# Forget gates of the second layer emitted beside band attention's third pair

## The chip, the cores and the metric

One core of a Trainium2 chip runs the whole program. Its engines work side by side, each through a queue of its own in fixed order: TensorE (PE) multiplies and transposes, VectorE (DVE), ScalarE (ACT) and GpSimd (POOL) do the elementwise work, and SyncE (SP) issues most of the DMA transfers. They wait for one another by semaphores. The metric is the device time of one execution in microseconds (us); lower is better.

## The reference

An encoder of two layers is run for 512 new frames of one stream (the prompt) and for the next 64 frames of another that has 1024 frames of history (the sample). The change lies in the second layer. Of its input projection the columns are cut into queries, keys, values and gates of two attentions of 8 heads each, "band" and "fox", and 8 columns for fox's forget values:

```python
q_c, k_c, v_c, g_c, q_d, k_d, v_d, f_d, g_d = split_cols(h @ w_in, ODD_SIZES)
log_f = jax.nn.log_sigmoid(f_d.astype(jnp.float32) + forget_bias.astype(jnp.float32))
...
cum = jnp.cumsum(log_f, axis=1)                                          # prompt
...
cum = jnp.cumsum(jnp.concatenate([p_lf.astype(jnp.float32), log_f], axis=1), axis=1)   # sample
...
s = s + (jnp.swapaxes(cum_q, 1, 2)[:, :, :, None] - jnp.swapaxes(cum_k, 1, 2)[:, :, None, :])
```

The running sums enter the scores of fox alone. `log_f` itself is an output.

## The kernel before

Every float32 product is made as three products of the operands' high and low parts, so a projection of one 128-wide tile is 48 matmuls: a bank of 256 frames (24 matmuls) and one of 320, the last 64 of them the sample's. Weights come by DMA into `wraw` (4 buffers); ACT makes the high part `whi` (L165) and POOL the low part `wlo` (L169), 5 buffers each.

The heads go by pairs, four for band and four for fox. For each pair there are projections (`band_qk` or `fox_qk`, matmuls at L252, evictions at L339 to L357), a gate tile (`gate_tile`, L252, evictions at L632 and L633), and the attention. The attention of a prompt pair (`head_out`) is a chain per 128 rows: scores (PE, L452, L453), bias and row minimum (DVE, L1227), exponential (ACT, L461), division (DVE, L463, L464), transposes (PE, L418), a split into two parts (ACT L421, DVE L422), then the product with the values (PE, L427). The sample's rows run beside it (L501 to L557). `v_chunk` projects two pairs' values, with matmuls at L262 (prompt) and L270 (sample).

What stands where is set twice. A scheduler orders each engine's queue by priority, and the attention of band and fox is emitted under a high one, so that projections emitted before or after it fill the places where the attention waits. Buffers of a ring, however, are handed out in the order in which the code asks for them. PSUM has two buffers each of `psA` (projections), `psS` (scores) and `psT` (transposes), one each of `psU` and `psX`. The ring "E" has five buffers of 2 KB rows, shared by `kf`, `kout`, `th`, `low`, `vf`, `cum` and `oT`.

The loop at L1278 runs over band's pairs p: `band_qk(p + 1)`, for p = 1 also the second value chunk, the gate tile, then the attention of pair p. Behind the loop stand fox's first value chunk (L1290) and the block that the change moves:

- the projection `w_vd1` of 264 columns: 256 values of fox and the 8 forget columns, four prompt tiles and the sample (96 and 16 matmuls), evicted at L1294, L1295, L282, L283, L1302, L1303;
- the logarithms (L1310 to L1319): ten small instructions on 128 x 40 numbers, turn by turn on ACT and DVE, with `Ln` at L1317, which needs a load of another ACT table, and two stores of the result (L1320, L1321);
- the running sums: PE transposes the log values into two `psT` banks (L1336, L1347), ACT copies them out (L1338, L1348), three loads bring the history's log values (`fox_lfT`, L1344), DVE makes one scan for the prompt and three chained ones for the sample (L1327), and each result is stored in DRAM (`cum_p`, `cum_s`, L1329).

Fox's attention reads them back as bias tiles `T` (`spread`, L1355). `fox_qk(0)` follows.

Of the kernel before, what the change touches and what calls it, by code (L numbers as in the profile page):

```python
# [10 lines left out]
F32 = mybir.dt.float32  # L11
F32R = mybir.dt.float32r
BF16 = mybir.dt.bfloat16
AF = mybir.ActivationFunctionType
ALU = mybir.AluOpType
AX = mybir.AxisListType

P = 128
D = 1024
KT = D // P  # L20
S = 512
NT = S // P
DS = 64
TT = S + DS
PAST = 1024
H = 8
# [33 lines left out]
def f32(ap):  # L60
    return ap.bitcast(F32)
# [3 lines left out]
def kernel(ctx: ExitStack, tc: tile.TileContext, a: dict, o: dict):  # L65
    nc = tc.nc
# [6 lines left out]
    dp = pool("dram", space=bass.MemoryType.DRAM)  # L73
# [3 lines left out]
    def nm(s):  # L77
        cnt[0] += 1
        return f"{s}_{cnt[0]}"
# [14 lines left out]
    def ring(shape, dt, tag, name=None):  # L94
        p, n = rings[tag]
        if isinstance(p, list):
            rings[tag][1] += 1
            return p[n % len(p)].tile(shape, dt, name=nm(name or tag), tag=tag, bufs=1)
        return p.tile(shape, dt, name=nm(name or tag), tag=tag, bufs=n)
# [4 lines left out]
    def Er(shape, name="e"):  # L104
        return ring(shape, F32, "E", name)
# [4 lines left out]
    def V2(shape, dt, name="v"):  # L110
        return ring(shape, dt, "V2", name)
# [4 lines left out]
    def bank(tag, bufs, n=512):  # L116
        return lambda: pp.tile([P, n], F32, name=nm("ps" + tag), tag=tag, bufs=bufs)

    psA, psS, psT, psU, psX = bank("A", 2), bank("S", 2), bank("T", 2), bank("U", 1), bank("X", 1)
# [5 lines left out]
    ident = cp.tile([P, P], F32, name="ident")  # L125
# [49 lines left out]
    def w_split(src, shape):  # L175
        return split(src, w_tile("wraw", shape, F32), w_tile("whi", shape, F32R), w_tile("wlo", shape, F32R))
# [45 lines left out]
    def bcast(src_row, n):  # L222
        return bass.AP(src_row.tensor, src_row.offset, [[0, P], [1, n]])
# [32 lines left out]
    def tm_prompt(ps, n, ws, h, ks, t):  # L256

        kp = KT // len(ws)
        for k in ks:
            hi, lo = ws[k // kp]  # L260
            for m, (x, w) in enumerate(((0, hi), (0, lo), (1, hi))):
                nc.tensor.matmul(ps[:, :n], h.m[k // 4][:, k % 4, x, t * P:(t + 1) * P], w[:, k % kp, :],  # L262
                                 start=(k == ks[0] and m == 0), stop=(k == ks[-1] and m == 2))

    def tm_sample(ps, n, ws, h, ks):

        kp = KT // len(ws)
        for k in ks:
            for m, w in enumerate(ws[k // kp]):
                nc.tensor.matmul(ps[:, :n], h.s[k // 4][:, k % 4, :], w[:, k % kp, :],  # L270
                                 start=(k == ks[0] and m == 0), stop=(k == ks[-1] and m == 1))

    def tm_chunk(ws, n, h, prompt_cb, sdst, ts=range(NT + 1)):

        for t in ts:
            ps = psA()
            if t < NT:
                tm_prompt(ps, n, ws, h, range(KT), t)
                prompt_cb(t, ps)
            else:  # L280
                tm_sample(ps, n, ws, h, range(KT))
                nc.scalar.copy(sdst, ps[DS:P, :n])  # L282
                nc.vector.tensor_add(sdst, ps[:DS, :n], sdst)  # L283

    def tm_weights(src):
        return [w_split(src[i], list(src[i].shape)) for i in range(4)]
# [99 lines left out]
    def put_v(dst, src):  # L386

        s4 = src.rearrange("p (a s d) -> p a s d", s=2, d=64)
        d4 = dst.rearrange("p a (s d) -> p a s d", s=4)[:, :, ::3, :]
        nc.vector.tensor_copy(out=d4, in_=s4)  # L390
        nc.vector.tensor_sub(dst[:, :, 64:192].rearrange("p a (s d) -> p a s d", s=2), s4, f32(d4))
# [226 lines left out]
    def gate_tile(src, h, ft, raw):  # L618
        g = bp.tile([P, TT], F32, name=nm("g"), tag=f"g{ft}", bufs=1)
        gates[ft] = g  # L620

        def cb(ps, c0, c1):
            n = c1 - c0
            gv = g[:, c0:c1]
            th = Er([P, 320], "th")
            tv = th[:, :n]
            if raw:
                nc.scalar.activation(tv, ps[:, :n], AF.Sigmoid)
                nc.vector.tensor_mul(gv, ps[:, :n], tv)
            else:  # L630

                nc.scalar.activation(tv, ps[:, :n], AF.Tanh, scale=0.5)  # L632
                nc.vector.scalar_tensor_tensor(out=gv, in0=tv, scalar=1.0, in1=ps[:, :n], op0=ALU.add, op1=ALU.mult)  # L633

        ws_tiles(h, ((src, cb, ()),))
# [134 lines left out]
    def load_x(t):  # L770
        rows = P if t < NT else DS
        x = [Rr([P, 512], "x") for _ in range(2)]
        for c in range(2):
            nc.sync.dma_start(f32(x[c][:rows]), xrow(t)[:, c * 512:(c + 1) * 512])
        return [f32(y) for y in x]
# [9 lines left out]
    x = load_x(0)  # L785
# [8 lines left out]
    for t in range(NT + 1):  # L794
# [7 lines left out]
        if t < NT:  # L802
            c0_weights(C0W[t])
            x = load_x(t + 1)
# [282 lines left out]
    t = psA()  # L1087
# [3 lines left out]
    for i in range(2):  # L1091
        raw = w_tile("wraw", [P, 512], F32)
        cs = slice(i * 512, (i + 1) * 512)
# [94 lines left out]
    h1 = new_h(big1)  # L1188
# [15 lines left out]
    l1 = new_pool(st_l1)  # L1204
    band, fox = new_mech(l1, "band"), new_mech(l1, "fox")
    fb = l1.tile([P, H], F32, name="fb")
    nc.scalar.dma_start(fb, bcast(a["d_forget_bias"], H))
    lf = l1.tile([P, NT + 1, H], F32, name="lf")
# [44 lines left out]
    def band_sample(p):  # L1253
# [10 lines left out]
                        lambda c: s_vals(a["band_v"][p], c, band.vn[:, p * P:(p + 1) * P]), s_new)  # L1264
        s_gate(s_fold(po, rs), gates[p])

    nc.sync.dma_start(npost, bcast(a["norm_post"][1:2, :], D))
    clear(band)
    clear_keys(band.kz)
# [8 lines left out]
    for p in range(NPAIR):  # L1278
        nxt = band_qk(p + 1) if p < 3 else None
        if p == 1:  # L1280
            v_chunk(band, 1, a["w_vc"][1], h1, o["p_bandv"])
        gate_tile(a["ws"][32 + p], h1, p, False)
        with tc.high_priority(PR_band):
            beside(band_sample(p), EV_band)
            band_pair(p, pr)
            drain()
        pr = nxt
    nc.sync.dma_start(o["s_bandv"][CL - DS:], band.vn)

    v_chunk(fox, 0, a["w_vd0"], h1, o["p_foxv"])  # L1290

    def vf_prompt(t, ps):
        vf = Er([P, 256], "vf")
        nc.scalar.copy(vf, ps[:, :256])  # L1294
        nc.vector.tensor_add(lf[:, t], ps[:, 256:264], fb)  # L1295
        nc.sync.dma_start(o["p_foxv"][t * P:(t + 1) * P, 256:], vf)
        fox.v[1, t] = V2([P, 2, 256], F32R)
        put_v(fox.v[1, t], vf)

    low = Er([P, 264], "low")  # L1300
    tm_chunk(tm_weights(a["w_vd1"]), 264, h1, vf_prompt, low[:DS])
    nc.vector.tensor_copy(out=fox.vn[:, 256:], in_=low[:DS, :256])  # L1302
    nc.vector.tensor_add(lf[:DS, NT], low[:DS, 256:264], fb[:DS])  # L1303
    nc.sync.dma_start(o["s_foxv"], fox.vn)


    lff = lf.rearrange("p t h -> p (t h)")
    NF = (NT + 1) * H
    e, u, w = (l1.tile([P, NF], F32, name=x) for x in ("lf_e", "lf_u", "lf_w"))
    nc.scalar.activation(e, lff, AF.Abs)  # L1310
    nc.scalar.activation(e, e, AF.Exp, scale=-1.0)
    nc.vector.tensor_scalar(out=u, in0=e, scalar1=1.0, scalar2=None, op0=ALU.add)
    nc.vector.tensor_scalar(out=w, in0=u, scalar1=-1.0, scalar2=None, op0=ALU.add)
    nc.vector.tensor_sub(e, e, w)
    nc.vector.reciprocal(w, u)
    nc.vector.tensor_mul(e, e, w)
    nc.scalar.activation(u, u, AF.Ln)  # L1317
    nc.vector.tensor_add(u, u, e)
    nc.vector.scalar_tensor_tensor(out=lff, in0=lff, scalar=0.0, in1=u, op0=ALU.min, op1=ALU.subtract)  # L1319
    nc.sync.dma_start(o["p_logf"].rearrange("(t p) h -> p t h", p=P), lf[:, :NT])  # L1320
    nc.sync.dma_start(o["s_logf"], lf[:DS, NT])  # L1321


    def running(parts, dst):
        carry, k = 0.0, 0
        for c, w in parts:
            nc.vector.tensor_tensor_scan(out=c[:H, :w], data0=c[:H, :w], data1=c[:H, :w], initial=carry,  # L1327
                                         op0=ALU.add, op1=ALU.bypass)
            nc.sync.dma_start(dst[:, k:k + w], c[:H, :w])  # L1329
            carry, k = c[:H, w - 1:w], k + w  # L1330

    cum_p = dp.tile([H, S], F32, name="cum_p")
    cum_s = dp.tile([H, PAST + DS], F32, name="cum_s")
    t = psT()
    for i in range(NT):
        nc.tensor.transpose(t[:H, i * P:(i + 1) * P], lf[:, i, :], ident)  # L1336
    c = Er([P, S], "cum")
    nc.scalar.copy(c[:H], t[:H])  # L1338
    running([(c, S)], cum_p)
    cs = []  # L1340
    for k in range(3):
        c = Er([P, 384], "cum")
        w = min(384, PAST - k * 384)
        nc.sync.dma_start(c[:H, :w], a["fox_lfT"][:, k * 384:k * 384 + w])  # L1344
        cs.append((c, w))
    t = psT()
    nc.tensor.transpose(t[:H, :DS], lf[:DS, NT, :], ident[:DS, :DS])  # L1347
    nc.scalar.copy(cs[2][0][:H, 256:256 + DS], t[:H, :DS])  # L1348
    cs[2] = (cs[2][0], 256 + DS)
    running(cs, cum_s)  # L1350

    def spread(dst, src, h, k0, n):

# [184 lines left out]
```

## Time and profile before

| | |
|---|---|
| runs | 835.79, 839.99, 846.00 us; median 839.99 |
| profiled execution | 844.3 us, of which the span of the trace is 842.5 |
| mean granted TensorE clock | 0.974 of full speed |
| PE busy | 776.0 us, 92% of the span |
| DVE busy | 506.7 us, 60% |
| ACT busy | 499.1 us, 59% |
| POOL busy | 380.1 us, 45% |

The engines overlap, so the busy times don't add up to the span. All times of single instructions below are from the profiled execution, counted from the start of its span; a matmul's own duration contains its way through the array, and consecutive ones overlap. Band's last pairs, the moved block and the start of fox lie between 540 and 670 us.

### The profile page before, as it was taken

What the parts mean: (1) busy time and instruction counts of PE and PEld (TensorE: products, weight loads), DVE (VectorE), ACT (ScalarE), POOL (GpSimd) and SP (SyncE); (2) the same over time, 40 slices, a digit from 0 to 9 for tenths busy, and PEclk for the clock granted to TensorE, in tenths of its full rate; (3) what the DMA queues carried; (4) which work ended last, traced back from release to release, by engine and by line L of the source; (5) the groups of instructions that cost most, each with busy time, mean ns of one, the idle gap of its engine ahead of it and who ended that gap; (6) DMA issues with size and microseconds to landing.
All of it is one profiled execution on the core that took longest, in us unless ns stands there. A gap on an engine that the chain in (4) does not pass through costs nothing. (4 is left out here: it accounts for less than half of the span.)

```text
span 842.5 us, 16286 instructions
## 1 busy us (share of the span) xinstructions
PE 776.0 (92%) x5581; PEld 720.4 (86%) x5581; DVE 506.7 (60%) x1318; ACT 499.1 (59%) x1342; POOL 380.1 (45%) x461
## 2 busy tenths in 40 slices
PE   7989999999998999889877999999997899999986
PEld 5879899999896888788876999999896799998986
DVE  4642755777855765837854555564754576658345
ACT  6643755677746675665543655575634767768521
POOL 6574533463417040154671545453245444546453
PEclk9989999999997999999998999999999999999999
DMA  8233423541123022246352544343233533551562
GB/s 244 76 112 96 141 68 107 182 124 55 43 78 100 23 52 78 60 122 213 113 160 69 154 106 116 110 133 88 70 95 102 180 123 110 159 140 56 164 213 100
DMA packets 69924, 95.52 MB, mean 113 GB/s; under 512 B 9529, under 2 KB 40489, under 8 KB 69810
## 3 DMA queue, kind: packets, MB, share of 16 engines
q1 hardware_dynamic: 69264, 94.12, 37.2%
q8 instruction: 44, 0.72, 0.3%
q10 hardware_dynamic: 578, 0.37, 0.1%
q14 instruction: 38, 0.31, 0.1%
HBM read 74.36 MB, written 18.79 MB: 111 GB/s over the span
## 5 line engine op out<-in xcount | busy, mean ns | idle before, releaser
L252 PE MATMUL psA<-hT,whi 128*128 128x320 f32 (+1 forms) x1216 | 259.1, 301 | 6.1 <-DVE r L340 2.2
L169 POOL TENSOR_TENSOR wlo<-wraw,whi 128x512 fp32r<-128x512 f32 (+2 forms) x130 | 167.6, 1299 | 196.6 <-ACT whi L165 155.0
L252 PEld LDWEIGHTS psA<-hT,whi 128*128 128x128 f32 x1216 | 198.6, 190 | 9.8 <-issue 4.1
L252 PE MATMUL psA<-hT,wlo 128*128 128x320 f32 (+1 forms) x608 | 183.3, 302 | 0.0
L262 PE MATMUL psA<-whi,hT 128*128 128x256 f32 (+2 forms) x812 | 163.8, 290 | 4.8 <-DVE m L737 2.2
L262 PEld LDWEIGHTS psA<-whi,hT 128*128 128x128 f32 x812 | 131.7, 191 | 7.2 <-DVE m L737 2.4
L262 PE MATMUL psA<-wlo,hT 128*128 128x256 f32 (+2 forms) x420 | 122.5, 292 | 0.0
L252 PEld LDWEIGHTS psA<-hT,wlo 128*128 128x128 f32 x608 | 115.6, 190 | 0.8
L165 ACT CAST whi<-wraw 128x512 fp32r<-128x512 f32 (+2 forms) x130 | 78.2, 615 | 42.1 <-PE psA L252 23.0
L262 PEld LDWEIGHTS psA<-wlo,hT 128*128 128x128 f32 x420 | 80.8, 192 | 0.8
L363 POOL TENSOR_TENSOR kz<-kf,r 64x256 fp32r<-64x256 f32 x48 | 36.6, 762 | 35.1 <-ACT kf L357 33.3
L422 DVE TENSOR_TENSOR pt1l<-psT,pt1h 128x384 fp32r<-128x384 f32 x64 | 39.7, 620 | 13.5 <-ACT pt1h L421 12.6
L1227 DVE CUSTOM_DVE_ANT_0 x<-psS,T 128x128 f32<-128x128 f32 (+1 forms) x64 | 31.0, 484 | 23.4 <-PE psT L418 8.5
L339 ACT ACTIVATE r<-psA 64x256 fp32r<-64x256 f32 x48 | 18.1, 378 | 41.1 <-PE psA L252 22.7
L533 POOL TENSOR_TENSOR sK<-kraw,sK 128x384 fp32r<-128x384 f32 (+2 forms) x32 | 30.1, 941 | 27.3 <-ACT sK L532 21.9
L461 ACT ACTIVATE psS<-x,st 128x128 f32<-128x128 f32 (+1 forms) x64 | 34.1, 532 | 13.7 <-DVE st L1227 13.3
L439 POOL TENSOR_TENSOR g<-g,oT 128x512 f32<-128x512 f32 x14 | 18.3, 1305 | 52.3 <-DVE oT L431 52.0
L421 ACT CAST pt1h<-psT 128x384 fp32r<-128x384 f32 x64 | 33.8, 530 | 13.3 <-PE psT L418 12.0
L520 PE MATMUL psX<-vs,sP 128*128 128x256 f32 (+1 forms) x184 | 38.6, 303 | 1.5 <-DVE sP L507 1.2
L431 DVE SCALAR_TENSOR_TENSOR oT<-psU,oT 64x256 f32<-64x256 f32 x64 | 26.8, 419 | 19.2 <-ACT oT L430 18.3
L452 PE MATMUL psS<-r,r 128*128 128x256 f32 (+1 forms) x96 | 35.1, 367 | 2.1 <-DVE st L1227 1.2
L430 ACT ACTIVATE oT<-psU 64x256 f32<-64x256 f32 x64 | 24.2, 378 | 21.7 <-PE psU L427 20.6
(390 smaller groups left out, 1915.6 us busy)
## 6 DMA issues: line engine op xcount, KB each, us to landing
wraw<-in_ws_dram SPq DMA_DIRECT2D x80, 256.0 KB
wraw<-in_w_out_dram SPq DMA_DIRECT2D x32, 256.0 KB
x<-in_x_prompt_dram SPq DMA_DIRECT2D x16, 256.0 KB
part<-part SPq DMA_DIRECT2D x32, 128.0 KB
m<-part SPq DMA_DIRECT2D x16, 256.0 KB
r<-r SPq DMA_DIRECT2D x48, 64.0 KB
out_dram<-kout SPq DMA_DIRECT2D x12, 256.0 KB
out_dram<-vf SPq DMA_DIRECT2D x24, 128.0 KB
```

Source lines behind the costliest of these rows:

```text
L165: nc.scalar.copy(hi, raw)
L169: eng.tensor_sub(lo, raw, f32(hi))
L252: nc.tensor.matmul(ps[:, :c1 - c0], w[:, k % 4, :], h.m[k // 4][:, k % 4, x, c0:c1], start=(k == 0 and n == 0), stop=(k == KT - 1 and n == 2))
L262: nc.tensor.matmul(ps[:, :n], h.m[k // 4][:, k % 4, x, t * P:(t + 1) * P], w[:, k % kp, :], start=(k == ks[0] and m == 0), stop=(k == ks[- ...
L363: nc.gpsimd.tensor_sub(pair.kl[s][me, cs], kf[me, cs], f32(k[me, cs]))
L421: nc.scalar.copy(ph[:, :i + 1, at], tv)
L422: nc.vector.tensor_sub(pl[:, :i + 1, at], tv, f32(ph[:, :i + 1, at]))
L452: nc.tensor.matmul(ps[:, :w], pair.qq[s][:, q], pair.kk[s][:, :w], start=True, stop=False)
L461: nc.scalar.activation(ps[:, :n], src, AF.Exp, bias=mn, scale=-1.0, accum_out=sm)
L520: nc.tensor.matmul(po[:, :256], l, r, start=(first and n == 0), stop=(last and n == len(ops) - 1))
L533: nc.gpsimd.tensor_sub(kl[:, :w], raw[:, :w], f32(kh[:, :w]))
L1227: nc.vector.tensor_tensor_reduce(out=x, in0=ps, in1=b, scale=1.0, scalar=3e38, op0=ALU.add, op1=ALU.min, accum_out=mn)
```

## The change

The block becomes a function `forget_gates()`, called in the loop over band's pairs at p = 2, behind that pair's gate tile and ahead of its attention. The two DRAM tiles and `vf_prompt` move up as they are. Inside, `running` now takes one chunk at a time: the load of `fox_lfT`, the scan and the store of a chunk are emitted in turn, and the carry is handed on. Fox's first value chunk now comes behind the second one, and so does the store `s_foxv` of the sample's values. The arithmetic is the same.

```diff
+    def forget_gates():
+        low = Er([P, 264], "low")
+        tm_chunk(tm_weights(a["w_vd1"]), 264, h1, vf_prompt, low[:DS])
...
+        nc.sync.dma_start(o["s_logf"], lf[:DS, NT])
+        def running(c, w, dst, k, carry):
+            nc.vector.tensor_tensor_scan(out=c[:H, :w], data0=c[:H, :w], data1=c[:H, :w], initial=carry,
+                                         op0=ALU.add, op1=ALU.bypass)
+            nc.sync.dma_start(dst[:, k:k + w], c[:H, :w])
+            return c[:H, w - 1:w]
+        t = psT()
+        for i in range(NT):
+            nc.tensor.transpose(t[:H, i * P:(i + 1) * P], lf[:, i, :], ident)
+        c = Er([P, S], "cum")
+        nc.scalar.copy(c[:H], t[:H])
+        running(c, S, cum_p, 0, 0.0)
+        carry = 0.0
+        for k in range(0, PAST, 384):
+            c = Er([P, 384], "cum")
+            w = min(384, PAST - k)
+            nc.sync.dma_start(c[:H, :w], a["fox_lfT"][:, k:k + w])
+            if k + w == PAST:
+                t = psT()
+                nc.tensor.transpose(t[:H, :DS], lf[:DS, NT, :], ident[:DS, :DS])
+                nc.scalar.copy(c[:H, w:w + DS], t[:H, :DS])
+                w += DS
+            carry = running(c, w, cum_s, k, carry)
...
         gate_tile(a["ws"][32 + p], h1, p, False)
+        if p == 2:
+            forget_gates()
         with tc.high_priority(PR_band):
...
     v_chunk(fox, 0, a["w_vd0"], h1, o["p_foxv"])
-    low = Er([P, 264], "low")
-    tm_chunk(tm_weights(a["w_vd1"]), 264, h1, vf_prompt, low[:DS])
...
-    running(cs, cum_s)
```

In the changed program the block's lines are L1275 for L1296, L1291 to L1300 for L1312 to L1321, L1304 for L1327, L1306 for L1329, L1311 and L1322 for L1336 and L1347, L1319 for L1344.

On PE, where the attention of band's third pair (p = 2) starts, its first transpose (the row L418) stood before among the projection of the fourth pair's queries:

```order
L427 MATMUL psU_7430<-pt0l,v_6136 128x256
L418 MATMUL psT_7773<-ident,x_7766 128x128
L252 MATMUL psA_7575<-hT_5393,whi_7564 128x256 x2
L452 MATMUL psS_7844<-r_6813,r_6810 128x384
L252 MATMUL psA_7575<-hT_5393,wlo_7565 128x256
L453 MATMUL psS_7844<-kz_5926,r_6810 128x384
```

Now four sets of scores of that pair stand ahead, then all of the block's 112 matmuls and the fourth pair's gate tile (the L252 rows) with nothing of the attention among them, and then this, with the first transpose behind those of the log values:

```order
L252 MATMUL psA_8247<-hT_5395,whi_8214 128x320 x2
L252 MATMUL psA_8247<-hT_5395,wlo_8215 128x320
L1311 MATMUL psT_7913<-ident,lf 8x128 x4
L1322 MATMUL psT_7932<-ident,lf 8x64
L418 MATMUL psT_7988<-ident,x_7981 128x128
L501 MATMUL psT_8001<-ident,sx_7940 128x128 x2
L520 MATMUL psX_7994<-vs_7998,sP_8004 128x256
L418 MATMUL psT_8023<-ident,x_8016 128x128 x2
```

The attention's transposes have changed places with the log values': they ask for `psT` banks behind them.

On DVE, the scans (printed as SCALAR_TENSOR_TENSOR) stood before among the evictions of fox's first queries:

```order
L1319 SCALAR_TENSOR_TENSOR lf<-lf,lf_u 128x40
L340 SCALAR_TENSOR_TENSOR r_8712<-psA_8758,r_8712 64x256
L345 SCALAR_TENSOR_TENSOR foxqbl<-psA_8758,foxqbh 64x64
L340 SCALAR_TENSOR_TENSOR r_8713<-psA_8758,r_8713 64x256
L1327 SCALAR_TENSOR_TENSOR cum_8690<-cum_8690 8x512
L345 SCALAR_TENSOR_TENSOR foxqbl<-psA_8758,foxqbh 64x64
L1327 SCALAR_TENSOR_TENSOR cum_8694<-cum_8694 8x384
L1327 SCALAR_TENSOR_TENSOR cum_8696<-cum_8696,cum_8694 8x384
```

Now they stand between rows of the third pair's softmax (the splits L422 and L507, the bias L1227):

```order
L1298 SCALAR_TENSOR_TENSOR lf<-lf,lf_u 128x40
L1304 SCALAR_TENSOR_TENSOR cum_7918<-cum_7918 8x512
L1227 ISA x_8092,st_8091<-psS_8088,T_7397 128x512
L1227 ISA st_8091 128x1
L422 TENSOR_TENSOR pt0l<-psT_7988,pt0h 128x128
L1304 SCALAR_TENSOR_TENSOR cum_7922<-cum_7922 8x384
L507 TENSOR_TENSOR sP_8005<-psT_8001,sP_8004 128x256
L1304 SCALAR_TENSOR_TENSOR cum_7926<-cum_7926,cum_7922 8x384
L463 RECIPROCAL st_8096<-st_8094 128x1
```

Each of the attention's rows there comes behind a scan.

On SP, the loads of the history's log values (L1319) stand behind the two stores of the new ones and a weight load for fox's first keys (`wraw_8797`):

```order
L160 DMA wraw_8791<-in_ws_dram 128x512
L1299 DMA out_dram<-lf 128x4x8
L1300 DMA out_dram<-lf 64x8
L160 DMA wraw_8797<-in_ws_dram 128x512
L1319 DMA cum_7922<-in_fox_lfT_dram 8x384
L1319 DMA cum_7926<-in_fox_lfT_dram 8x384
L1319 DMA cum_7930<-in_fox_lfT_dram 8x256
L1306 DMA cum_p<-cum_7918 8x512
L1217 DMA T_8288<-in_relb_dram 64x256 x2
```

Before, they stood behind the same stores and two later weight loads; behind them now wait bias rows of band's fourth pair (`T`, L1217).

## Rows read from the trace of the kernel before

**Rows 1.** Windows: stretch, its length, busy us (and instructions) by engine, PEclk, DMA.
```profile
592.39:598.07 5.68, 4.93 (x32) 3.76 (x31) 5.48 (x21) 4.62 (x15) 1.28 (x1) 1.00 0.04 10
598.07:625.67 27.60, 27.60 (x222) 26.79 (x221) 16.25 (x51) 13.57 (x36) 7.43 (x8) 1.00 0.30 90
625.67:649.19 23.52, 18.67 (x132) 16.66 (x131) 14.29 (x23) 11.51 (x28) 16.89 (x20) 1.00 0.30 88
649.19:662.00 12.81, 10.18 (x70) 9.35 (x71) 5.13 (x19) 7.13 (x18) 3.36 (x3) 1.00 0.68 203
```

**Rows 2.** Timeline of PE: start, duration, engine, line, operation, [idle before <-releaser].
```profile
625.54 0.29 PE L270 MATMUL psA<-wlo,hsT 128*128 128x264 f32 x1
625.67 0.40 PE L252 MATMUL psA<-hT,whi 128*128 128x256 f32 x2
628.50 0.45 PE L252 MATMUL psA<-hT,whi 128*128 128x320 f32 x2
631.86 0.31 PE L252 MATMUL psA<-hT,wlo 128*128 128x320 f32 x1
```

**Rows 3.** Groups of PE instructions by form, 625.67 to 662.
```profile
L252 PE MATMUL psA<-hT,whi 128*128 128x256 f32 x64 | 12.3, 288 | 2.3 <-DVE r L340 2.2
L252 PE MATMUL psA<-hT,whi 128*128 128x320 f32 x52 | 11.6, 311 | 2.0 <-DVE foxqbl L345 2.0
L252 PE MATMUL psA<-hT,wlo 128*128 128x256 f32 x32 | 9.2, 286 | 0.0
L252 PE MATMUL psA<-hT,wlo 128*128 128x320 f32 x25 | 7.7, 308 | 0.0
```

**Rows 4.** Waits of PE, 600 to 690: us in total, times, longest us.
```profile
PE psA L252 <- DVE r L340: 2.2, 2, 1.2
PE psA L252 <- DVE foxqbl L345: 2.0, 2, 1.3
PE psS L452 <- DVE st L1227: 1.2, 1, 1.2
PE psA L374 <- ACT kf L357: 1.1, 1, 1.1
```

**Rows 5.** Timeline of DVE, forget gates' chain and scans.
```profile
627.37 1.39 DVE L1302 COPY foxvn<-low 64x256 f32<-64x256 f32 x1
630.28 1.22 DVE L1313 TENSOR_SCALAR lf_w<-lf_u 128x40 f32<-128x40 f32 x1
631.52 0.42 DVE L340 SCALAR_TENSOR_TENSOR r<-psA,r 64x256 fp32r<-64x256 f32 x1
633.10 1.32 DVE L1316 TENSOR_TENSOR lf_e<-lf_e,lf_w 128x40 f32<-128x40 f32 x1
637.45 1.21 DVE L1327 TENSOR_TENSOR_SCAN cum<-cum 8x512 f32<-8x512 f32 x1 [0.17 <-ACT cum L1338]
639.80 0.95 DVE L1327 TENSOR_TENSOR_SCAN cum<-cum 8x384 f32<-8x384 f32 x1 [0.88 <-DMA cum<-in_fox_lfT_dram]
640.84 3.04 DVE L1327 TENSOR_TENSOR_SCAN cum<-cum,cum 8x384 f32<-8x384 f32 x2
```

**Rows 6.** Timeline of POOL in the same stretch.
```profile
628.90 2.55 POOL L169 TENSOR_TENSOR wlo<-wraw,whi 128x512 fp32r<-128x512 f32 x2
633.08 1.29 POOL L169 TENSOR_TENSOR wlo<-wraw,whi 128x512 fp32r<-128x512 f32 x1 [1.06 <-ACT whi L165]
```

**Rows 7.** Timeline of PE: transposes of the log values.
```profile
635.29 0.60 PE L1336 MATMUL psT<-ident,lf 128*8 128x128 f32 x4
```

**Rows 8.** Timeline of ACT: the copy out of PSUM.
```profile
636.84 0.57 ACT L1338 COPY cum<-psT 8x512 f32<-8x512 f32 x1
```

**Rows 9.** Windows of two us around a gap in layer 0, columns as in rows 1.
```profile
444.00:446.00 2.00, 0.61 (x6) 0.38 (x4) 1.93 (x5) 2.00 (x6) 0.00 (x0) 1.00 0.59 229
446.00:448.00 2.00, 0.00 (x0) 0.00 (x0) 1.30 (x3) 0.55 (x2) 0.86 (x2) 0.66 0.28 98
450.00:452.00 2.00, 2.00 (x9) 1.55 (x8) 1.38 (x2) 1.43 (x4) 0.18 (x1) 0.50 0.44 131
```

More of the change, by code (lines that the diff above doesn't have):

```diff
@@ L1265, in band_sample, with vf_prompt @@
         s_gate(s_fold(po, rs), gates[p])
+    cum_p = dp.tile([H, S], F32, name="cum_p")
+    cum_s = dp.tile([H, PAST + DS], F32, name="cum_s")
+    def vf_prompt(t, ps):
+        vf = Er([P, 256], "vf")
+        nc.scalar.copy(vf, ps[:, :256])
+        nc.vector.tensor_add(lf[:, t], ps[:, 256:264], fb)
+        nc.sync.dma_start(o["p_foxv"][t * P:(t + 1) * P, 256:], vf)
+        fox.v[1, t] = V2([P, 2, 256], F32R)
+        put_v(fox.v[1, t], vf)
+    def forget_gates():
+        low = Er([P, 264], "low")
+        tm_chunk(tm_weights(a["w_vd1"]), 264, h1, vf_prompt, low[:DS])
+        nc.vector.tensor_copy(out=fox.vn[:, 256:], in_=low[:DS, :256])
+        nc.vector.tensor_add(lf[:DS, NT], low[:DS, 256:264], fb[:DS])
+        lff = lf.rearrange("p t h -> p (t h)")
+        NF = (NT + 1) * H
+        e, u, w = (l1.tile([P, NF], F32, name=x) for x in ("lf_e", "lf_u", "lf_w"))
+        nc.scalar.activation(e, lff, AF.Abs)
+        nc.scalar.activation(e, e, AF.Exp, scale=-1.0)
+        nc.vector.tensor_scalar(out=u, in0=e, scalar1=1.0, scalar2=None, op0=ALU.add)
+        nc.vector.tensor_scalar(out=w, in0=u, scalar1=-1.0, scalar2=None, op0=ALU.add)
+        nc.vector.tensor_sub(e, e, w)
+        nc.vector.reciprocal(w, u)
+        nc.vector.tensor_mul(e, e, w)
+        nc.scalar.activation(u, u, AF.Ln)
+        nc.vector.tensor_add(u, u, e)
+        nc.vector.scalar_tensor_tensor(out=lff, in0=lff, scalar=0.0, in1=u, op0=ALU.min, op1=ALU.subtract)
+        nc.sync.dma_start(o["p_logf"].rearrange("(t p) h -> p t h", p=P), lf[:, :NT])
+        nc.sync.dma_start(o["s_logf"], lf[:DS, NT])
[21 more added lines that the diff above has]
+            carry = running(c, w, cum_s, k, carry)
@@ L1290 @@
     v_chunk(fox, 0, a["w_vd0"], h1, o["p_foxv"])
[L1292 to L1298, printed above, removed]
-    low = Er([P, 264], "low")
-    tm_chunk(tm_weights(a["w_vd1"]), 264, h1, vf_prompt, low[:DS])
-    nc.vector.tensor_copy(out=fox.vn[:, 256:], in_=low[:DS, :256])
@@ L1303 @@
-    nc.vector.tensor_add(lf[:DS, NT], low[:DS, 256:264], fb[:DS])
-    nc.sync.dma_start(o["s_foxv"], fox.vn)
[L1307 to L1349, printed above, removed]
-    running(cs, cum_s)
+    nc.sync.dma_start(o["s_foxv"], fox.vn)
     def spread(dst, src, h, k0, n):
```

## The prediction

> **What bounds the kernel now.** PE is busy nearly all the time, so I read the stretch around the moved block by PE alone: first the windows, which say how many matmuls each stretch gets through, then PE's timeline and waits, which say what stops it, then the queues of DVE, ACT and POOL behind the longest stop.
>
> The windows [rows 1] show three kinds of stretch. In 598.07 to 625.67, the projections of fox's values with band's last attention dissolved in them, PE has no gap: 222 matmuls in 27.60 us, 0.124 us each. In 592.39 to 598.07 attention stands bare, with no projection between its matmuls: 32 in 5.68 us, 0.178 each, while DVE is busy for 5.48 us of it with 21 instructions, 0.26 each. There DVE is the bound. And from 625.67 to 662.00, where the forget gates' logarithms and sums run beside fox's first projections, PE has gaps.
>
> How large these are: the projection's 256-column matmuls start 0.118 us apart (24 from 625.67 to 628.50) and the 320-column ones 0.146 apart (23 from 628.50 to 631.86) [rows 2]. In 625.67 to 662.00 there are 64 + 32 of the first and 52 + 25 of the second [rows 3], and 132 + 70 in all [rows 1], so 29 others. The work is 96 x 0.118 + 77 x 0.146 + 29 x 0.124 = 11.3 + 11.2 + 3.6 = 26.1 us of 36.33. So **10.2 us are idle**. What ends these waits is the eviction of fox's queries by DVE (2.2 and 2.0 us), a softmax row (1.2) and the eviction of keys by ACT (1.1) [rows 4]. The evictions are late because the forget chain stands ahead of them on the same engines: 1.39, 1.22 and 1.32 us for three DVE rows of the logarithms [rows 5], and 1.21 + 0.95 + 3.04 = 5.2 us of scans [rows 5]. In the bare stretch the same reckoning gives 5.68 - 32 x 0.124 = 1.7 us idle.
>
> **The change, part by part.** No arithmetic is added. The 112 matmuls, the logarithms, the four scans and the table load for the logarithm run once in either kernel. So the sum is over PE's idle time, from band's third pair to the start of fox.
>
> *Taken away.* The hole of 10.2 us loses the forget chain. What stays is what fox's start has for itself: the keys' eviction (1.1), the first softmax row (1.2) [rows 4] and some 0.7 for the rest, an estimate; 3.0 in all. Gain 7.2 us. The bare stretch at 592 to 598 goes too, since the third pair's attention no longer ends there: gain 1.7 us.
>
> *Added: the third pair's attention waits for the forget gates.* This is the main term, and the order of the instructions shows it: the transposes of the log values ask for the two `psT` banks ahead of the attention's, so the first L418 of the pair stands behind L1311 and L1322 on PE. From the last sample matmul of the moved projection to these transposes nothing is on PE but the fourth pair's gate tile. Before, that chain took from 625.54 + 0.29 [rows 2] to 635.29 [rows 7], 9.5 us; two evictions of fox's queries (L340, 0.42 each [rows 5]) stood in it and won't now, so 8.6. Then the transposes 0.6 [rows 7], the copy 0.6 [rows 8], the scans 5.2, and a wait for the history's load, 0.9 as before the second scan [rows 5], because the loads still stand on SP behind the stores of the result. Between the scans DVE's queue has some fifteen rows of softmax before it reaches the eviction of the gate tile for which fox's first value tile waits: 15 x 0.26 = 3.9 us. In all 19.8 us. In this time PE has the gate tile, 24 x 0.118 + 24 x 0.146 = 6.3 us, and 26 matmuls of attention, 3.2 us. So **10.3 us idle**. Bounds: 4.4, if the three slow DVE rows take 0.3 each (-3.0), there is no wait for the load (-0.9) and half the softmax rows fall into waits (-2.0); 13, if the loads are held for two POOL rows more (2.55 [rows 6]).
>
> *Added: the clock.* After PE did nothing in 446 to 448, it ran in 450 to 452 at a granted clock of 0.50, the lower of the two levels, 1.2 GHz, with 9 matmuls in 2 us [rows 9]. Such a gap of some us now comes in the third pair's attention, behind the gate tile. Four us at half clock cost 2.0 us; bounds 0 (in all of 625.67 to 662.00, with its 10.2 us idle, the clock stayed at 1.00 [rows 1]) and 3.5.
>
> *Added: a longer bare stretch.* The held attention is made up later: behind the first two tiles of fox's value chunk come 74 matmuls of the third and fourth pairs with no projection between them, since the third tile of that chunk finds no free buffer and fox's queries come behind it. At 0.178 each they take 13.1 us, for 74 x 0.124 = 9.2 us of work: 3.9 us idle, between 3 and 7 (the last if DVE's scans reach into it).
>
> *At nothing.* From fox's first product with the values on, both orders have the same work in the same sequence. The store `s_foxv` and the stores of the log values wait for nobody on the path; the second table load stays one, 1.28 us on ACT, in the shadow of the same waits.
>
> Sum: -7.2 - 1.7 + 10.3 + 2.0 + 3.9 = **+7.3 us**. The profiled execution took 844.3, so 851.6; it lies 4.3 above the median of 840.0, and the same difference on the median gives **847.3 us**.
>
> **The rivals.** *It is about even.* The three slow DVE rows are not slow by themselves: 630.28 + 1.22 and 633.10 + 1.32 end within 0.05 us of the POOL rows of the weights' low parts (628.90 + 2.55, 633.08 + 1.29) [rows 5, 6], so DVE is held there by POOL. Where no weight is being split in that moment they take some 0.3 us, and the chain is 3.0 us shorter. The clock may hold, as it did at 625 to 662 (-2.0), and the wait for the load vanish behind the first scan and a softmax row (-0.9). Then the sum is +7.3 - 5.9 = +1.4: 841.4. The Trainium skill, "SBUF — State Buffer", section "SBUF: two separate sides", says that DVE and GpSimd share one port pair under an exclusive lock, and that the one that comes second blocks fully for the whole instruction. The trace agrees: each of these rows ends with the POOL row, 0.05 us apart. By that rule what the logarithms cost in their new place hangs on whether POOL has weights to split there; it has those of fox's values, which speaks for the slow rows.
>
> *Faster.* The hole closes and nothing opens: -7.2 - 1.7 = -8.9, 831.1. It needs the third pair's attention to find cover for the 19.8 us of its wait, thus work on PE beside the 9.5 us that the order puts there. For it speaks that PE had no gap in 598 to 625, where attention stood among projections, and that the hole is real; against it the order, which can't be passed on an in-order queue.
>
> *Slower still.* The loads of the history's log values stand on SP behind a weight load (`wraw_8797`) whose buffer comes free only when POOL has split an earlier weight, which itself stands behind the `Ln` and its table load on ACT. If they are held for two POOL rows (2.55 us [rows 6]), scans and softmax rows on DVE's queue wait as long, PE's gap grows and the clock falls a second time (+2.0), and the sum is +11.9: 851.9. It decides as soon as the loads leave SP over 2 us behind the stores of the log values.
>
> *The change doesn't do what it says* is excluded by the order: the block stands where the change puts it.
>
> **How the numbers follow.** Forecast 0.40, even 0.25, slower still 0.18, faster 0.17. A measurement of this kernel can tell about 1% (8.4 us) from no change: 831.6 and 848.4. The forecast lies next to the upper of these, and its terms have bounds on both sides, so half of it counts as slower: slower 0.20 + 0.18 = 0.38; same 0.20 + 0.25 = 0.45; faster 0.17. The range goes from 833, a little above the faster case, to 856, which is the slower one with the bare stretch at its upper bound (+3.1, rounded up); some 0.1 is left out below and as much above.
>
> **What would show it.** Right: in the profile after, no L418 of band's third pair between the last L262 or L270 of the moved projection and L1311; behind the gate tile a gap of some 10 us on PE, ended by DVE or ACT; half clock in a window or two behind it; a piece of attention with some 0.18 us for each matmul; and no gap over 1.5 us at fox's first queries. Wrong: if PE's gap before L1311 is under 5 us, the chain was shorter than I read it; if the hole at fox's start stays, the forget chain was not its cause.

## The result, and the profile of the changed kernel

The changed kernel takes 845.12 us in the median of 20 runs, the kernel before 839.16 in as many beside it. The ratio is 1.0054, with a 95% interval of 1.0034 to 1.0074: slower by some 4.5 us (the two medians differ by 6.0), less than the 7.3 forecast and on the same side.

The profiled execution of the changed kernel took only 841.2 us, with a span of 839.3, less than the 844.3 shown before. Single executions of either kernel differ by some 10 us, and here it is time ahead of the change that differs: at the first value product (L427) of band's first pair the changed kernel's execution is already 6.7 us earlier (475.46 against 482.20). Of this, 3.7 us come ahead of the program's first L427, where the mean granted clock was 0.982 against 0.949, and 3.2 in the last 100 us ahead of band, at 0.975 against 0.924. So stretches of the two traces are compared between the same instructions. From the first L427 of band's second pair to the last L427 of fox the work is the same: before it lasts from 525.98 to 792.65, 266.7 us, and after from 519.27 to 790.83, 271.6 us, +4.9. Of this, +3.3 had come by the first L427 of fox (140.6 against 143.9 us); of the 1.6 behind it, the six more matmuls that stand behind that point are some 0.7, and the rest isn't explained. This execution has the highest mean granted clock of the changed kernel's 20, 0.983; their median is 0.9755, where the kernel before has medians of 0.978 to 0.980 in the runs beside the experiments. In most executions the clock thus loses more than this trace shows; where in the span isn't known.

These are windows of the changed kernel, cut at the places that the prediction speaks of: from the end of the moved projection to fox's first value tile (L262), its first two tiles, the piece of attention behind them, the rest of the tiles, and fox's queries and keys up to fox's first L427.

```profile
577.70:594.27 16.57, 13.08 (x81) 11.28 (x80) 12.77 (x30) 10.85 (x27) 7.45 (x7) 0.90 0.44 117
594.27:601.46 7.19, 7.19 (x55) 6.71 (x54) 2.95 (x11) 1.52 (x5) 0.00 (x0) 1.00 0.06 17
601.46:617.41 15.95, 12.76 (x75) 9.61 (x75) 13.49 (x49) 11.56 (x35) 4.40 (x6) 1.00 0.23 70
617.41:640.00 22.59, 22.59 (x175) 21.76 (x176) 12.42 (x35) 13.49 (x37) 9.53 (x14) 1.00 0.48 135
640.00:663.13 23.13, 21.79 (x156) 20.20 (x155) 11.53 (x40) 15.05 (x43) 13.91 (x15) 1.00 0.46 131
```

The first has 81 matmuls in 16.57 us and a mean granted clock of 0.90, and the third 75 in 15.95 us, 0.213 each, with DVE busy for 13.49 us. The other three run at 0.129 to 0.148 each, nearer to the 0.124 of the stretch without gaps [rows 1]. The timeline of PE at the first, with idle time in brackets:

```profile
577.58 0.29 PE L270 MATMUL psA<-wlo,hsT 128*128 128x264 f32 x1
577.70 0.40 PE L252 MATMUL psA<-hT,whi 128*128 128x256 f32 x2
...
583.92 0.31 PE L252 MATMUL psA<-hT,wlo 128*128 128x320 f32 x1
584.07 0.60 PE L1311 MATMUL psT<-ident,lf 128*8 128x128 f32 x4
...
585.43 0.33 PE L418 MATMUL psT<-ident,x 128*128 128x128 f32 x1 [0.62 <-ACT cum L1313]
...
586.44 0.39 PE L520 MATMUL psX<-vs,sP 128*128 128x256 f32 x1 [0.46 <-ACT sP L506]
588.45 0.41 PE L418 MATMUL psT<-ident,x 128*128 128x128 f32 x2 [1.62 <-DVE pt0l L422]
589.53 1.01 PE L520 MATMUL psX<-vs,sP 128*128 128x256 f32 x3 [0.68 <-DVE sP L507]
```

The gate tile (the L252 rows) reaches from 577.70 to 584.07, and the log values' transposes follow it without a gap: the logarithms were ready. Behind them PE waits for the copy of the log values out of PSUM (0.62), then for softmax rows on ACT and DVE (0.46, 1.62, 0.68), with little in between. No L418 stands between the moved projection and L1311. DVE in the same stretch:

```profile
579.46 0.28 DVE L1282 COPY foxvn<-low 64x256 f32<-64x256 f32 x1
579.67 1.25 DVE L1283 TENSOR_TENSOR lf<-low,fb 64x8 f32<-64x8 f32 x1
...
581.49 0.70 DVE L1291 TENSOR_SCALAR lf_u<-lf_e 128x40 f32<-128x40 f32 x1 [0.57 <-ACT lf_e L1290]
582.22 0.18 DVE L1292 TENSOR_SCALAR lf_w<-lf_u 128x40 f32<-128x40 f32 x1
...
583.11 0.20 DVE L1295 TENSOR_TENSOR lf_e<-lf_e,lf_w 128x40 f32<-128x40 f32 x1
...
585.47 2.04 DVE L1304 TENSOR_TENSOR_SCAN cum<-cum 8x512 f32<-8x512 f32 x1 [1.61 <-ACT cum L1313]
```

Against [rows 5], the copy of the sample's values (L1282) took 0.28 instead of 1.39, and the two rows that took 1.22 and 1.32 took 0.18 (L1292) and 0.20 (L1295). Now L1283 takes 1.25 and the first scan (L1304) 2.04 instead of 1.21; L1291 is slow in both, 0.70 and 0.71. The two rows of the kernel before that [rows 5] leaves out:

```profile
628.68 0.28 DVE L1303 TENSOR_TENSOR lf<-low,fb 64x8 f32<-64x8 f32 x1
629.53 0.71 DVE L1312 TENSOR_SCALAR lf_u<-lf_e 128x40 f32<-128x40 f32 x1 [0.57 <-ACT lf_e L1311]
```

So these five rows of the logarithms' chain take 2.6 us where they took 4.9. POOL tells why:

```profile
577.01 5.13 POOL L169 TENSOR_TENSOR wlo<-wraw,whi 128x512 fp32r<-128x512 f32 x4 [11.54 <-ACT whi L165]
583.93 2.50 POOL L169 TENSOR_TENSOR wlo<-wraw,whi 128x512 fp32r<-128x512 f32 x2 [1.79 <-ACT whi L165]
```

Four weights are split from 577.01 to 582.14 and two from 583.93 to 586.43. L1291 ends at 582.19, 0.05 us behind the first four; L1292 to L1298 fall into the pause; the scan begins beside the last of the two and ends 1.08 us behind it.

The clock behind the gap, in windows of two us (the granted clock is the third number from the end of a row):

```profile
588.00:590.00 2.00, 0.88 (x4) 0.67 (x5) 2.00 (x6) 1.13 (x3) 0.00 (x0) 0.88 0.14 35
590.00:592.00 2.00, 2.00 (x11) 1.96 (x11) 2.00 (x7) 1.26 (x5) 0.28 (x1) 0.50 0.48 69
592.00:594.00 2.00, 1.89 (x11) 1.37 (x9) 2.00 (x8) 1.61 (x5) 0.23 (x1) 0.77 0.43 144
```

It stands at 0.50, the lower level (1.2 GHz), for some 3.4 us, which is 0.24 + 1.0 + 0.46 = 1.7 us lost. In the kernel before no window of this stretch is below 1.00 [rows 1]. At fox's start the waits of [rows 4] are nearly gone; these are the largest up to fox's second queries:

```profile
645.41 0.38 PE L452 MATMUL psS<-r,r 128*128 128x256 f32 x1 [0.26 <-DVE st L1227]
...
646.24 0.44 PE L374 MATMUL psA<-ident,kf 128*128 128x128 f32 x2 [0.25 <-ACT kf L357]
...
647.30 0.45 PE L555 MATMUL psS<-sK,foxqbh 128*128 128x384 f32 x1 [0.42 <-POOL sK L533]
```

So both halves of the forecast are in the trace: the hole at fox's start closes, and a hold, a fall of the clock and a long bare piece of attention open in front of it.

### The profile page after: what moved, and what is told of

It is laid out like the page before. It is cut to its first block, busy times and chain, and to the rows that moved or that the text cites. A ratio compares the mean times of both kernels' runs of the same rounds, so it can differ in the third digit from the quotient of the medians.

```text
span 839.3 us, 16283 instructions
## 1 busy us (share of the span) xinstructions
PE 772.9 (92%) x5581; PEld 714.7 (85%) x5581; DVE 501.6 (60%) x1318; ACT 498.9 (59%) x1342; POOL 379.3 (45%) x461
## 5 line engine op out<-in xcount | busy, mean ns | idle before, releaser
L252 PE MATMUL psA<-hT,whi 128*128 128x320 f32 (+1 forms) x1216 | 257.7, 300 | 2.7 <-ACT kf L357 2.2
L252 PEld LDWEIGHTS psA<-hT,whi 128*128 128x128 f32 x1216 | 198.1, 190 | 4.9 <-ACT kf L357 2.9
L252 PE MATMUL psA<-hT,wlo 128*128 128x320 f32 (+1 forms) x608 | 182.2, 300 | 0.0
L262 PE MATMUL psA<-whi,hT 128*128 128x256 f32 (+2 forms) x812 | 161.3, 287 | 5.0 <-DVE m L737 2.3
L262 PEld LDWEIGHTS psA<-whi,hT 128*128 128x128 f32 x812 | 129.7, 188 | 7.7 <-DVE m L737 2.3
L262 PE MATMUL psA<-wlo,hT 128*128 128x256 f32 (+2 forms) x420 | 121.5, 289 | 0.0
L252 PEld LDWEIGHTS psA<-hT,wlo 128*128 128x128 f32 x608 | 115.2, 189 | 0.6
L262 PEld LDWEIGHTS psA<-wlo,hT 128*128 128x128 f32 x420 | 79.7, 190 | 0.8
L422 DVE TENSOR_TENSOR pt1l<-psT,pt1h 128x384 fp32r<-128x384 f32 x64 | 39.7, 621 | 13.7 <-ACT pt1h L421 12.6
L1227 DVE CUSTOM_DVE_ANT_0 x<-psS,T 128x128 f32<-128x128 f32 (+1 forms) x64 | 30.9, 482 | 22.0 <-PE psS L453 10.9
```

The lines of the kernel that those rows point to most:

```text
L252: nc.tensor.matmul(ps[:, :c1 - c0], w[:, k % 4, :], h.m[k // 4][:, k % 4, x, c0:c1], start=(k == 0 and n == 0), stop=(k == KT - 1 and n == 2))
L422: nc.vector.tensor_sub(pl[:, :i + 1, at], tv, f32(ph[:, :i + 1, at]))
L1227: nc.vector.tensor_tensor_reduce(out=x, in0=ps, in1=b, scale=1.0, scalar=3e38, op0=ALU.add, op1=ALU.min, accum_out=mn)
```

## The experiments

The theory: the loss comes from the **hold**. The third pair's transposes get their PSUM banks behind those of the log values, so its attention stands still until the logarithms are done and is then made up bare. The rival: **used-up fillers**. The projection, once emitted earlier, is missing as cover beside the fourth pair and at fox's start, whatever is held. The table gives every kernel: median, ratio to the kernel before with its interval, and the length of the stretch from the second pair's first L427 to fox's last in the profiled execution (before 266.7 us).

| kernel | median us | ratio | stretch us |
|---|---|---|---|
| the change | 845.12 | 1.0054 (1.0034 to 1.0074) | 271.6 |
| sums behind the third pair | 844.14 | 1.0055 (1.0031 to 1.0080) | 270.5 |
| transposes in the projections' banks | 849.82 | 1.0121 (1.0088 to 1.0155) | 276.8 |
| transposes in the sample's bank | 846.86 | 1.0080 (1.0049 to 1.0111) | 273.5 |
| the block at the fourth pair | 837.93 | 0.9969 (0.9945 to 0.9992) | 264.7 |
| no hold | 836.33 | 0.9954 (0.9927 to 0.9981) | 262.3 |
| sums behind, own buffers | 838.26 | 0.9971 (0.9946 to 0.9995) | 264.7 |
| fourth pair, sums last | 839.41 | 0.9996 (0.9975 to 1.0018) | 264.8 |
| turns only | 839.59 | 0.9993 (0.9969 to 1.0017) | 267.4 |
| the change, own buffers | 844.25 | 1.0043 (1.0025 to 1.0060) | 270.7 |
| early | 834.06 | 0.9918 (0.9888 to 0.9948) | 260.9 |
| late | 834.86 | 0.9917 (0.9895 to 0.9940) | 260.5 |
| fourth pair, own buffers | 839.40 | 0.9975 (0.9953 to 0.9998) | 265.8 |

The kernel before ran beside each later group of four: its median was 840.85 us beside the first four runs, 839.80 beside the next and 841.36 beside the last, so kernels of different groups are compared by their ratios. The stretch, from one execution of each, follows the ratios within some 2 us, which ties the differences to this part of the program.

**Sums behind the third pair's attention.**

```diff
+    def forget_sums():
         def running(c, w, dst, k, carry):
...
             drain()
+        if p == 2:
+            forget_sums()
         pr = nxt
```

> The projection and the logarithms stay beside band's third pair, ahead of its attention; the transposes and the running sums are emitted behind that attention, so its transposes no longer ask for PSUM banks behind those of the log values. If the held attention is the cost of the change, its hole (some 8 us idle, 2 of half clock) and the bare stretch behind it go, while the gain at fox's start stays: 833 to 837 us, faster than before by 0.3 to 0.7%. If the cost is only that fillers are used up earlier, the time stays near the change's, 843 to 846.

It measured 844.1: as the rival had it. The trace shows another reason. The third pair now mixes with the projection, but the sums' transposes stand ahead of the fourth pair's, and the hold has only moved. PE there:

```profile
596.21 0.39 PE L452 MATMUL psS<-r,r 128*128 128x256 f32 x1 [0.90 <-DVE st L1227]
...
598.33 0.33 PE L418 MATMUL psT<-ident,x 128*128 128x128 f32 x1 [1.24 <-ACT cum L1314]
...
602.28 0.55 PE L427 MATMUL psU<-pt1h,v 128*128 128x256 f32 x1 [1.59 <-DVE oT L431]
```

The scans came late because the loads of the history stood on SP (issues: start, duration) behind a weight load that began 3.45 us after the store ahead of it:

```profile
592.54 0.52 SPq L1300 DMA_DIRECT2D out_dram<-lf  x1
595.99 0.33 SPq L160 DMA_DIRECT2D wraw<-in_ws_dram  x1
596.37 1.04 SPq L1320 DMA_DIRECT2D cum<-in_fox_lfT_dram  x3
```

And there is a second loss at fox's first keys:

```profile
639.13 0.57 PE L252 MATMUL psA<-hT,whi 128*128 128x320 f32 x2 [2.54 <-ACT kf L357]
```

This wait of 2.54 us ends with ACT, but ACT's row had waited for DVE, whose queue stood full of value splits, one of them of 1.52 us, before it reached the query's eviction (L340):

```profile
631.94 1.52 DVE L391 TENSOR_TENSOR v<-vf,v 128x256 fp32r<-128x256 f32 x1
...
636.57 0.42 DVE L340 SCALAR_TENSOR_TENSOR r<-psA,r 64x256 fp32r<-64x256 f32 x1
```

So a hole at fox's start can come from other rows than the forget gates', and this run could not decide. The clock fell behind both places; the median granted clock of its eight executions is 0.972, against 0.978 for the kernel before beside them, some 5 us of 840 at most, as much as the whole loss.

**The log values' transposes in other banks.** Each of the eight PSUM buffers that the kernel's pools hold has its use, and the log values' transposes got none of their own. One run took the projections' buffers, one the sample products' single one (`psX` for `psA` in the same two lines).

```diff
-        t = psT()
+        t = psA()
         for i in range(NT):
...
-                t = psT()
+                t = psA()
```

> As the change, but the log values' transposes take their two banks from the projections' PSUM buffers instead of the transposes' ones. The third pair's attention is free; the fourth pair's gate tile waits for the logarithms instead. Held attention as the cause: the wait moves to the gate tile, with some 4 us idle ahead of the log values' transposes, and the long bare stretch goes: 836 to 841 us. Used-up fillers as the cause: 843 to 846.

> As the change, but the log values' transposes take the one bank of the sample's value products. The prompt's attention of the third pair goes on up to the next sample step, and only the sample's part is held. Held attention as the cause: between the change and the run with the projections' banks, 839 to 844 us. Used-up fillers: 843 to 846, and no difference from the change.

Both missed: 849.8, clearly slower than the change, and 846.9, no faster than it. The hold goes where the bank goes. With the projections' buffers it is the gate tile, the only filler there, that waits for the logarithms, and the clock falls for longer:

```profile
586.00:588.00 2.00, 0.35 (x4) 0.11 (x1) 2.00 (x5) 0.39 (x2) 2.00 (x2) 0.93 0.73 214
588.00:590.00 2.00, 1.48 (x5) 1.20 (x6) 1.80 (x8) 0.47 (x2) 0.46 (x2) 0.50 0.48 156
```

(The windows up to 600 are at 0.50 too.) With the sample's bank it is the sample's products that stand still, and PE with them:

```profile
593.69 1.75 PE L520 MATMUL psX<-vs,sP 128*128 128x256 f32 x5 [3.74 <-DVE vs L547]
```

That a bank chosen for its neighbours is no better than the one in the change fits a price of the hold, but the numbers expected were wrong.

**The whole block one pair later.**

```diff
-        if p == 2:
+        if p == 3:
             forget_gates()
```

> The block is called one pair later, beside band's fourth pair, ahead of its attention. The same hold, on the fourth pair, with fox's first two value tiles (40 matmuls, 5 us) beside the logarithms in place of the gate tile. Held attention: no better than before by more than 2 us, 839 to 845 us. Used-up fillers: the fillers stand one pair later than in the change, so better than it by half of its loss or more, 836 to 841.

837.9: faster than before, in the range that I had given to the rival. The same hold is there, with 48 matmuls of fox's first value tiles (L262) beside it, and so are its waits (0.52, 0.46 and, as the longest, 1.68) and a fall of the clock that costs the same 1.7 us (rows below, at the last run):

```profile
605.32 0.66 PE L418 MATMUL psT<-ident,x 128*128 128x128 f32 x2 [1.68 <-DVE pt0l L422]
```

What differs is what comes behind it: the rest of fox's values and its queries are left as cover. So the hold and its clock alone don't make the loss; it takes a held piece of attention that finds no cover behind, which is the part of the rival that is true.

**No hold.**

```diff
-            nc.tensor.transpose(t[:H, i * P:(i + 1) * P], lf[:, i, :], ident)
+            nc.tensor.transpose(t[:H, i * P:(i + 1) * P], lfc[:, i * H:(i + 1) * H], ident)
...
-        c = Er([P, S], "cum")
-        nc.scalar.copy(c[:H], t[:H])
+        nc.scalar.copy(own[2][:H], t[:H])
```

> As the change, with no hold at all: the transposes read a constant instead of the log values, so the running sums do not depend on the logarithms (that part of the computation is left out), the sums have buffers of their own and the history is loaded at the second pair. Projection, logarithms, scans and stores are all still run. Held attention as the cause of the loss: the third pair mixes with the moved projection, no bare stretch, the gain at fox's start stays: 833 to 838 us. Used-up fillers as the cause (the projection is missing beside the fourth pair and at fox's start, whatever is held): 842 to 846.

836.3, in the theory's range: the same work at the same place in the code, without the wait and with buffers of its own (their part is measured below), is 1.0% faster than the change, more than the whole loss. This is what the rival can't give. The transposes and the last two scans run at 553 to 558 us there, ahead of everything that the change held.

**Sums behind, with buffers of their own.** The edit is that of the first run with the buffers of the one before (`own`, three gate buffers that fox uses later), and real log values.

> As the run with the sums behind the third pair's attention, but with buffers of their own for the sums (three that fox's last gates use later) and the history loaded at the second pair; two scans over the history instead of three. If in that run the fourth pair was held by the late loads and by the ring's buffers, its hole near the sums (gaps of 1.2, 0.5 and 1.6 us, and some 2.5 us of half clock) goes: 838 to 841 us. If fillers are the cause: 843 to 845, as that run.

838.3, 0.8% below the first run by their ratios, in the range expected. The trace gives most of it another place than I had: PE's waits around the sums (0.90, 1.24, 0.46 and 1.59 in the first run) only fall to 0.40, 0.49, 1.44 and 0.47, while those at fox's start (2.54, 1.04, 0.72 and 1.43) are gone but for 0.48 and 0.40. Whether loads or ring did it isn't shown.

**Projection and logarithms at the fourth pair, sums last.**

```diff
-        if p == 2:
+        if p == 3:
             forget_gates()
...
     nc.sync.dma_start(o["s_foxv"], fox.vn)
+    forget_sums()
```

> Projection and logarithms beside the fourth pair, ahead of its attention; transposes and sums behind fox's first values, as in the kernel before. Nothing is held, and the logarithms are off fox's start. Held attention: 832 to 836 us, better than the block as a whole beside the fourth pair (838). Fillers: about the same as that run, 837 to 839.

839.4, no better than before: the theory's number was missed. Nothing is held, but the hole at fox's start is all there, with the logarithms gone from it:

```profile
621.60 0.56 PE L252 MATMUL psA<-hT,whi 128*128 128x320 f32 x2 [1.35 <-DVE foxvn L283]
...
628.09 0.48 PE L252 MATMUL psA<-hT,whi 128*128 128x256 f32 x2 [2.73 <-DVE r L340]
...
632.83 0.56 PE L252 MATMUL psA<-hT,whi 128*128 128x320 f32 x2 [1.70 <-ACT kf L357]
...
638.46 0.44 PE L374 MATMUL psA<-ident,kf 128*128 128x128 f32 x2 [1.12 <-ACT kf L357]
```

So it was not the logarithms that made this hole, as I had read it; value splits and sums on DVE's queue, ahead of the query's eviction, are enough. In the longest of these waits PE does nothing for two us, and the clock stays at 1.00:

```profile
626.00:628.00 2.00, 0.00 (x0) 0.00 (x0) 1.85 (x4) 1.00 (x2) 0.54 (x2) 1.00 0.18 64
```

**Turns only.** In the kernel before, load, scan and store of each chunk in turn:

> The kernel before with one part of the change alone: load, scan and store of each chunk of the running sums are emitted in turn. Both theories: no difference that can be told, 838 to 842 us. If the order of the loads mattered by itself, over 843.

```diff
-    cs = []
-    for k in range(3):
+    carry = 0.0
+    for k in range(0, PAST, 384):
...
-    running(cs, cum_s)
+        carry = running(c, w, cum_s, k, carry)
```

839.6, no difference: this part of the change does nothing to the time.

**The change with buffers of its own.** The buffers alone, with the history loaded at the second pair and scanned in two pieces, the first of them at 455 us; everything else as in the change:

```diff
         if p == 1:
+            own_loads()
             v_chunk(band, 1, a["w_vc"][1], h1, o["p_bandv"])
```

> The change with buffers of their own for the sums and the history loaded early, and nothing else moved: the third pair's transposes still wait for the logarithms. If the wait for the logarithms is most of the hold's cost, 842 to 844 us, a part of the loss gone; if the late loads and the ring's buffers were it, 836 to 839, as in the run without a hold.

844.3, just above what was expected: ratio 1.0043 against the change's 1.0054. Ring and loads count for little here. And the run without a hold has these buffers too and differs from this one only in what the transposes read: 0.9954 against 1.0043, so 0.9% hangs on the wait for the log values.

**Early and late.** Two versions that leave the hold out with all data used: between the logarithms and their transposes stand projections that don't need the banks.

```diff
+            own_loads()
...
         gate_tile(a["ws"][32 + p], h1, p, False)
         if p == 2:
-            forget_gates()
+            forget_sums()
         with tc.high_priority(PR_band):
...
             drain()
+        if p == 1:
+            forget_gates()
```

> Projection and logarithms behind the second pair's attention, ahead of the fourth pair's queries and keys; transposes and sums beside the third pair as in the change, with buffers of their own. The order puts 48 matmuls of queries between the last sample matmul and the transposes, so nothing should be held, with all the data used. Held attention as the cause: 833 to 838 us. Fillers: 842 or more, since the projection stands earlier still.

The late one has 3 for 2 and 2 for 1:

> Projection and logarithms behind the third pair's attention, transposes and sums behind the fourth pair's gate tile, with buffers of their own. Gate tile and half a value tile, 58 matmuls or some 7 us, stand ahead of the transposes: a hold of 0 to 2 us. Held attention: 834 to 838 us. Fillers: 837 to 840.

834.1 and 834.9, both 0.8% faster than before and 1.3% faster than the change. The early one moves the projection further ahead than the change does, where the rival wanted 842 or more. With this the rival falls as a cause by itself. The early one's last two scans (577.08 and 578.41) still stand beside the third pair's attention, so scans among its softmax rows are not the cost by themselves either. The largest gaps of the early one on PE, around the sums:

```profile
574.67 0.39 PE L452 MATMUL psS<-r,r 128*128 128x256 f32 x1 [0.64 <-DVE x L464]
...
575.80 0.53 PE L252 MATMUL psA<-hT,whi 128*128 128x320 f32 x2 [0.63 <-DVE bandqbl L345]
...
581.21 0.44 PE L374 MATMUL psA<-ident,kf 128*128 128x128 f32 x2 [1.12 <-ACT kf L357]
```

They stay apart, and though PE is idle for over half of two windows, the clock stays at 1.00:

```profile
574.00:576.00 2.00, 0.73 (x4) 0.52 (x4) 1.34 (x5) 1.15 (x4) 0.00 (x0) 1.00 0.63 220
580.00:582.00 2.00, 0.88 (x7) 0.66 (x6) 1.61 (x6) 1.95 (x7) 2.00 (x2) 1.00 0.04 8
```

**The block at the fourth pair, with buffers of its own.**

> The block beside the fourth pair, with buffers of their own for the sums and the history loaded early. The hold of some 5 us of logarithms beside 40 matmuls stays, the waits for scans and loads behind it go: 1 to 3 us below that run (838), 835 to 837 us. If it stays at 838, neither ring nor loads counted there.

839.4 and a ratio of 0.9975, the same as without (0.9969): a miss. The waits of the hold stay as they were, and the longest is no shorter:

```profile
607.95 0.66 PE L418 MATMUL psT<-ident,x 128*128 128x128 f32 x2 [1.91 <-DVE pt0l L422]
```

In the profiled execution the clock costs more, too. It is at the lower level over these windows,

```profile
606.00:608.00 2.00, 0.09 (x2) 0.08 (x2) 2.00 (x5) 1.27 (x2) 0.00 (x0) 0.56 0.08 15
608.00:610.00 2.00, 2.00 (x10) 1.96 (x11) 1.54 (x7) 1.73 (x8) 0.00 (x0) 0.50 0.07 22
610.00:612.00 2.00, 2.00 (x11) 2.00 (x11) 1.55 (x8) 1.04 (x5) 0.00 (x0) 0.50 0.38 105
612.00:614.00 2.00, 2.00 (x11) 1.71 (x10) 1.67 (x6) 1.74 (x7) 0.00 (x0) 0.74 0.58 193
```

which lose 0.88 + 1.0 + 1.0 + 0.52 = 3.4 us, against 0.58 + 1.0 + 0.12 = 1.7 without the buffers:

```profile
604.00:606.00 2.00, 0.68 (x4) 0.71 (x5) 1.98 (x6) 1.32 (x3) 0.00 (x0) 0.71 0.10 18
606.00:608.00 2.00, 2.00 (x11) 1.96 (x11) 2.00 (x7) 1.63 (x6) 0.00 (x0) 0.50 0.06 14
608.00:610.00 2.00, 2.00 (x14) 1.67 (x13) 2.00 (x8) 1.56 (x5) 0.00 (x0) 0.94 0.24 85
```

Over the twelve executions of each the median granted clock is the same (0.978 and 0.977), so the clock is not shown to be the reason of the miss.

## Why the prediction was right, point by point

The forecast, its mechanism and its place hold: a hold by the transposes' banks, a fall of the clock, a bare stretch, against the hole at fox's start. Its sizes don't all, and two misses of opposite sign largely cancel: that the sum came as near as it did is in part luck.

- **The signs.** No L418 ahead of L1311, half clock behind the hold, bare attention and no gap over 1.5 us at fox's start are as forecast. The gap of some 10 us is not there, and one of the prediction's own signs of being wrong is: a gap of under 5 us before L1311 was to mean that the chain was shorter than read, and there is none at all. The sum itself had only 8.6 - 6.3 = 2.3 us there and the rest of the gap behind.

- **The hole at fox's start** (-7.2). The waits of 6.5 us in [rows 4] have become some 1.3 us. By the prediction's reckoning 116 projection matmuls and 37 others start in the last of the windows above: 23.13 - 48 x 0.118 - 68 x 0.146 - 37 x 0.124 = 2.9 us are idle, where 3.0 was to stay, so the gain is about the one forecast. The reason was only half right: the run with the sums last shows that the hole needs no logarithms, only vector work ahead of the evictions. That it closed in the change owes more to the scans and splits having moved.
- **The hold** (+10.3) **and the clock** (+2.0). From 577.87 to 594.27 it lasted 16.4 us where I had 19.8. Idle are 16.57 - 6.4 (gate tile) - 30 x 0.124 = 6.5 us, the clock's 1.7 among them, where I had 12.3. The term that was mis-sized most is the chain of the logarithms: 577.87 to 584.07, 6.2 us against 8.6, so the gate tile covered it whole. Another 2 us of the difference is that the prediction put the clock's loss on top of the hold's length, where the measured 16.4 us contain it. I took the durations of [rows 5] as the logarithms' own and priced their dependence on POOL only in the lower bound and in a rival. That rule (the Trainium skill, "SBUF — State Buffer", section "SBUF: two separate sides": whichever of DVE, in a 2-port mode or with two SBUF inputs against a GpSimd row that reads SBUF, and GpSimd starts first has the shared port pair for its whole instruction, and the other blocks fully) is borne out by the rows above: 0.18 and 0.20 in POOL's pause, 2.04 for a scan that began beside a POOL row.
- **The bare stretch** (+3.9, between 3 and 7). 75 matmuls in 15.95 us, for 75 x 0.124 = 9.3 of work: 6.7 us, next to the upper bound. 0.178 a matmul, taken from a short stretch, was too little; it was 0.213, with DVE busy for 85%. Three of the 32 matmuls of that short stretch only reach into it; by the 29 that start in it it is 0.196.
- **Sum.** -7.2, -1.7 (as forecast, not measured by itself), +6.5 and +6.7 make some +4.3 by its own terms; the traces give +3.3 up to fox's first product and +4.9 to its last, the runs +4.5. The hold with its clock was taken some 6 us too large and the bare stretch 3 us too small.
- **The rivals.** "About even" had the mechanism of the short rows right, and the time wrong, because the clock did fall and the bare stretch was longer. "Slower still": the loads left SP 0.8 us behind the stores (585.62, the last store's issue ending at 584.84), and nothing of it came. "Faster" needed cover for the third pair's wait; the early and the late version give it that, and come to 834 to 835 us.

What stays open is what makes the clock fall: the early version's idle windows and a gap of 2.73 us in the run with the sums last left it at 1.00, shorter gaps in the change did not. The prediction's term for it stood on one gap in layer 0 [rows 9]; that it came so near (1.7 for 2.0) is luck as well, and over all executions it may be larger.

## What to carry to other kernels

Where buffers are handed out in program order, a short chain that asks for one ahead of a high-priority stage holds that stage, whatever the priorities say: put independent work between the chain and the point where its buffer is asked for, as the early and late versions did, or see that cover is left behind the hold, as at the fourth pair. Moving such a buffer to another pool moves the hold to that pool's next user. A stretch of attention that is held and finds no cover comes back bare: here at 0.213 us a matmul, and that cost 6.7 us, as much as the hold itself with its clock (6.5).

## What was not expected of the hardware

Two gaps alike in PE's timeline cost differently by what the clock did behind them: gaps of 1.68 and 1.91 us (the block at the fourth pair, without and with buffers of its own) were followed by 1.7 and 3.4 us lost at the lower level, while in the early version windows with PE idle for 1.27 and 1.12 of 2 us, and a gap of 2.73 us in the run with the sums last, cost nothing more. A scan of 8 x 512 numbers took 2.04 us when it began beside a POOL row and 1.21 in the kernel before.
